# Loads of two, four and two rows per partition in place of four and four, with stores of two rows from the same ring

## The chip, the cores and the metric

One core of one Trainium2 chip runs the kernel. The metric is the device time of one execution in microseconds (us), the median over several runs. All runs in this document are with a granted clock of 1.0. Each kernel was also profiled once. The span in a profile, from the first to the last instruction, is about 1.8 us shorter than the device time. The packet durations below come from this one profiled execution of each kernel.

Terms: HBM is the chip's main memory, SBUF the core's own memory with 128 partitions. A DMA is a transfer between or within them, done by 16 DMA engines. A ring is the queue of transfers that one issuing engine (here SP, or SyncE) fills. A packet is the piece of a transfer that one DMA engine moves at a time, as the trace records it.

## The reference

```python
def reference(x, axis):                      # x: 1024 x 4096, float32; axis = -1
    mean = np.mean(x, axis=axis, keepdims=True)
    return ((x - mean) ** 2).astype(np.float32)
```

The input and the output are 16.78 MB each. Every row of 4096 elements (16 KiB) needs its mean before its first output element can be made.

## The kernel before

The 1024 rows are two tiles of 128 partitions, with four consecutive rows per partition. Both tiles are loaded first, with one DMA each. For each of the four row columns of a tile, VectorE (DVE) makes the negative sum and the negative mean, and ScalarE (ACT) squares x minus the mean in place. After every two rows a store goes out. All loads and stores are issued by SP, so they stand in one ring.

```python
x_t = x.rearrange("(n p q) d -> n p (q d)", p=P, q=Q)       # Q = 4, two tiles
out_t = out.rearrange("(n p q) d -> n p (q d)", p=P, q=Q)
...
for i in range(ntiles):
    x_tile = io.tile([P, Q * D], F32)
    nc.sync.dma_start(out=x_tile, in_=x_t[i])
...
        nc.vector.reduce_sum(out=neg_sum, in_=row, ..., negate=True)
        nc.vector.tensor_scalar_mul(out=neg_mean, in0=neg_sum, scalar1=inv_d)
        nc.scalar.activation(out=row, in_=row, func=Square, bias=neg_mean, scale=1.0)
        if q % H == H - 1:                                   # H = 2
            part = slice((q + 1 - H) * D, (q + 1) * D)
            nc.sync.dma_start(out=out_t[i][:, part], in_=tiles[i][:, part])
```

## Time and profile before

| | before |
|---|---|
| device time, median (lowest to highest) | 83.22 us (83.12 to 83.38, 3 runs; with a fourth run 83.19 us) |
| span | 81.3 us |
| DVE, ACT busy | 35.4 us, 30.7 us |
| DMA queue, share of 16 engines' span | 96.2% |
| first reduction starts | 22.50 us |
| first store issued | 39.46 us |
| loads landed | 22.5 and 41.8 us |

The share of the queue is the row to look at first. The prediction below shows the lines themselves. One more view is needed for what follows: the loads by their tensor. Its last line gives the time from issue to landing, as minimum, median and maximum over the loads. Before:

```profile
L43 SPq DMA_DIRECT2D x_tile<-in_x_dram x2: 382/404/425, 0.7 to 1.2; - x2
DMA to landing us min/median/max: 21.7/31.2/40.6
```

The second load is issued at 1.16 us and lands 40.6 us later, at 41.8 us. In the trace all load packets start before the first store packet does, so this moment is where the loads end and the stores begin.

### The profile page before, as it was taken

The page shows a single profiled execution, that of the slowest core. Times are in us where ns is not written, and L with a number is a line of the kernel's source. Part 1 is how long each engine was busy: PE and PEld are TensorE (multiplying, and loading weights), DVE is VectorE, ACT ScalarE, POOL GpSimd, SP SyncE. Part 2 cuts the span into 40 slices and gives each one's busy share as a digit, 9 for nine tenths or more (in the row PEclk, how much of TensorE's full clock was granted, in tenths as well). Part 3 has the DMA queues.
Part 4 walks back from the last instruction along what each step waited for, and adds up shares of the span by engine and source line. Part 5 has one row for each costly group of instructions (what it writes and reads, how often), then busy time and mean ns, then how long its engine had stood idle before and what let it go on. Part 6 is the DMA issues. An engine that isn't in the chain of part 4 may idle for free.

```text
span 81.3 us, 79 instructions
## 1 busy us (share of the span) xinstructions
DVE 35.4 (44%) x16; ACT 30.7 (38%) x9; POOL 0.2 (0%) x4
## 2 busy tenths in 40 slices
DVE  0000000000099999999749999999920000000000
ACT  0000000000060005969699930979879980000000
POOL 0000000000000000000000000000000000000000
DMA  9399947999965999992997997997998998898990
GB/s 387 129 516 516 516 193 322 516 516 516 516 290 226 516 516 516 516 483 129 419 516 306 467 516 322 451 516 338 435 516 354 419 516 387 387 516 387 403 500 0
DMA packets 864, 33.55 MB, mean 413 GB/s; under 512 B 96, under 2 KB 96, under 8 KB 96
## 3 DMA queue, kind: packets, MB, share of 16 engines
q1 hardware_dynamic: 864, 33.55, 96.2%
HBM read 16.78 MB, written 16.78 MB: 412 GB/s over the span
## 4 chain that ended last, share of the span: by engine, by line
DMA 50%; DVE 22%; ACT 5%; ACTq 4%; SPq 0%; issue 0%
DMA x_tile<-in_x_dram 50%; DVE neg_sum L51 21%; ACT x_tile L55 5%; ACTq L95 4%; SPq L43 0%; DVE neg_mean L54 0%
## 5 line engine op out<-in xcount | busy, mean ns | idle before, releaser
L51 DVE TENSOR_REDUCE neg_sum<-x_tile 128x1 f32<-128x4096 f32 x8 | 35.0, 4413 | 24.1 <-DMA x_tile<-in_x_dram 24.1
L55 ACT ACTIVATE x_tile<-x_tile,neg_mean 128x4096 f32<-128x4096 f32 x8 | 29.4, 3704 | 13.5 <-DVE neg_mean L54 13.5
L55 ACT ACT_TABLE_LOAD x1 | 1.3, 1283 | 22.5 <-DMA x_tile<-in_x_dram 22.5
L54 DVE TENSOR_SCALAR neg_mean<-neg_sum 128x1 f32<-128x1 f32 x8 | 1.1, 148 | 0.0
L81 POOL MEMSET const-bfloat16-1.0<- 128x1 bf16 x1 | 0.1, 101 | 0.0
L81 POOL MEMSET const-uint8-127<- 128x1 uint8 x1 | 0.1, 101 | 0.0
L81 POOL MEMSET const-float32-0.0<- 128x1 f32 x1 | 0.1, 98 | 0.2 <-issue 0.2
L81 POOL MEMSET const-float32-1.0<- 128x1 f32 x1 | 0.1, 98 | 0.0
## 6 DMA issues: line engine op xcount, KB each, us to landing
out_dram<-x_tile SPq DMA_DIRECT2D x4, 4096.0 KB, 12.9
x_tile<-in_x_dram SPq DMA_DIRECT2D x2, 31.2
```

The source lines that it names most:

```text
L51: nc.vector.reduce_sum(out=neg_sum, in_=row, axis=mybir.AxisListType.X, negate=True)
L54: nc.vector.tensor_scalar_mul(out=neg_mean, in0=neg_sum, scalar1=inv_d)
L55: nc.scalar.activation(out=row, in_=row, func=mybir.ActivationFunctionType.Square, bias=neg_mean, scale=1.0,)
L81: nc = _bacc.Bacc("TRN2", target_bir_lowering=False, num_devices=1)
L95: with _tile.TileContext(nc) as tc:
```

## The change

The intent is to let the engines start earlier: with a first load of half the size, DVE has its first two rows in half the time. The rows are laid out anew to make that possible. A partition now owns eight consecutive rows (a pitch of 128 KiB), of which the loads take two, four and two.

```diff
-    Q = 4
-    H = 2
+    R = B // P
+    LOADS = [2, 4, 2]
+    S = 2
...
-    x_t = x.rearrange("(n p q) d -> n p (q d)", p=P, q=Q)
+    x_v = x.rearrange("(p r) d -> p (r d)", p=P)
...
+    for i, n in enumerate(LOADS):
+        x_tile = io.tile([P, n * D], F32, tag=f"x{i}")
+        nc.sync.dma_start(out=x_tile, in_=x_v[:, r0 * D:(r0 + n) * D])
+        rows += [(x_tile, k) for k in range(n)]
+        r0 += n
...
+        if r % S == S - 1:
+            nc.sync.dma_start(
+                out=out_v[:, (r + 1 - S) * D:(r + 1) * D],
+                in_=x_tile[:, (k + 1 - S) * D:(k + 1) * D],
             )
```

(The sum, the mean and the square of each row are as before.)

More of the change, by code (lines that the diff above doesn't have):

```diff
@@ L27 @@
     P = nc.NUM_PARTITIONS
-    Q = 4
-    H = 2
-    assert B % (P * Q) == 0
-    ntiles = B // (P * Q)
+    R = B // P
+    LOADS = [2, 4, 2]
+    S = 2
+    assert B == P * R and sum(LOADS) == R
     inv_d = 1.0 / float(D)
-    x_t = x.rearrange("(n p q) d -> n p (q d)", p=P, q=Q)
-    out_t = out.rearrange("(n p q) d -> n p (q d)", p=P, q=Q)
-    io = ctx.enter_context(tc.tile_pool(name="io", bufs=ntiles))
-    stats = ctx.enter_context(tc.tile_pool(name="stats", bufs=2 * ntiles * Q))
-    tiles = []
@@ L41 @@
-    for i in range(ntiles):
-        x_tile = io.tile([P, Q * D], F32)
-        nc.sync.dma_start(out=x_tile, in_=x_t[i])
-        tiles.append(x_tile)
-    for i in range(ntiles):
-        for q in range(Q):
-            row = tiles[i][:, q * D:(q + 1) * D]
-            neg_sum = stats.tile([P, 1], F32)
-            neg_mean = stats.tile([P, 1], F32)
-            nc.vector.reduce_sum(
-                out=neg_sum, in_=row, axis=mybir.AxisListType.X, negate=True
-            )
-            nc.vector.tensor_scalar_mul(out=neg_mean, in0=neg_sum, scalar1=inv_d)
-            nc.scalar.activation(
-                out=row,
-                in_=row,
-                func=mybir.ActivationFunctionType.Square,
-                bias=neg_mean,
-                scale=1.0,
-            )
-            if q % H == H - 1:
-                part = slice((q + 1 - H) * D, (q + 1) * D)
-                nc.sync.dma_start(out=out_t[i][:, part], in_=tiles[i][:, part])
+    x_v = x.rearrange("(p r) d -> p (r d)", p=P)
@@ new lines @@
+    out_v = out.rearrange("(p r) d -> p (r d)", p=P)
+    io = ctx.enter_context(tc.tile_pool(name="io", bufs=1))
+    stats = ctx.enter_context(tc.tile_pool(name="stats", bufs=2 * R))
+    rows = []
+    r0 = 0
+    for i, n in enumerate(LOADS):
[3 more added lines that the diff above has]
+        r0 += n
+    for r, (x_tile, k) in enumerate(rows):
+        row = x_tile[:, k * D:(k + 1) * D]
+        neg_sum = stats.tile([P, 1], F32)
+        neg_mean = stats.tile([P, 1], F32)
+        nc.vector.reduce_sum(
+            out=neg_sum, in_=row, axis=mybir.AxisListType.X, negate=True
+        )
+        nc.vector.tensor_scalar_mul(out=neg_mean, in0=neg_sum, scalar1=inv_d)
+        nc.scalar.activation(
+            out=row,
+            in_=row,
+            func=mybir.ActivationFunctionType.Square,
+            bias=neg_mean,
+            scale=1.0,
+        )
+        if r % S == S - 1:
+            nc.sync.dma_start(
+                out=out_v[:, (r + 1 - S) * D:(r + 1) * D],
+                in_=x_tile[:, (k + 1 - S) * D:(k + 1) * D],
+            )
```

## The prediction

> **What bounds the kernel now.** I read the page first: the engines' busy time, the DMA row of the 40 slices, and the queue.
>
> ```profile
> span 81.3 us, 79 instructions
> ...
> DVE 35.4 (44%) x16; ACT 30.7 (38%) x9; POOL 0.2 (0%) x4
> ...
> DMA  9399947999965999992997997997998998898990
> ...
> q1 hardware_dynamic: 864, 33.55, 96.2%
> HBM read 16.78 MB, written 16.78 MB: 412 GB/s over the span
> ```
>
> No compute engine is busy for half of the span; the one DMA queue is busy for 96.2% of it. The low digits in the DMA row look like pauses, but a digit counts a large packet in the slice where it was recorded, so neighbouring digits trade with each other. To see whether the pauses are real I cut the span at the moments when the traffic starts, changes from loads to stores and ends, and then the store half into pieces of one store each (window; then its length and the busy time of DVE, ACT and POOL; the last three numbers are the TensorE clock, the DMA share and GB/s):
>
> ```profile
> 1.83:41.50 39.67, 17.71 (x8) 10.09 (x4) 0.00 (x0) 1.00 1.00 430
> 41.50:80.20 38.70, 17.71 (x8) 20.64 (x6) 0.00 (x0) 1.00 0.97 420
> ...
> 41.50:51.20 9.70, 9.37 (x4) 6.45 (x3) 0.00 (x0) 1.00 1.00 432
> 51.20:60.90 9.70, 8.34 (x5) 8.34 (x3) 0.00 (x0) 1.00 1.00 432
> 60.90:70.60 9.70, 0.00 (x0) 5.85 (x2) 0.00 (x0) 1.00 1.00 432
> ```
>
> The pauses are gone: the DMA share is 1.00 from the first byte to 70.6 us, at 430 to 432 GB/s. The packet records of the trace say the same: 256 load packets of 64 KiB (median 2.418 us) and 512 store packets of 32 KiB (median 1.213 us). All their times, summed and divided by 16 engines, are 78.2 us, and the traffic runs from 1.83 to 80.2 us, 78.4 us. The transfers fill the span with next to no hole.
>
> Then I read the chain of waits, which seems to say otherwise:
>
> ```profile
> 1.16 40.64 DMA x_tile<-in_x_dram
> ...
> 41.83 8.75 DVE neg_sum L51 x2
> ...
> 59.45 3.71 ACT x_tile L55
> 63.15 3.60 ACTq L95
> ```
>
> It is a chain through the second load, the four reductions of the second tile and the last squares. But it ends at 66.8 us, 14.5 us before the span does: the landing of the last stores is not in it. The waits of SP's own queue have it: at the end of the kernel SP stands 13.3 us for the stores.
>
> ```profile
> SPq L95 <- DMA out_dram<-x_tile: 13.3, 2, 9.6
> ```
>
> So what matters of the engine chain is one thing only: does each store reach the queue before the queue runs dry? The timeline of SP, taken store by store, gives the issue time and the time to landing:
>
> ```profile
> 39.46 0.35 SPq L64 DMA_DIRECT2D out_dram<-x_tile  x1
> DMA to landing us min/median/max: 12.1/12.1/12.1
> 47.45 0.34 SPq L64 DMA_DIRECT2D out_dram<-x_tile  x1
> DMA to landing us min/median/max: 13.8/13.8/13.8
> 58.79 0.33 SPq L64 DMA_DIRECT2D out_dram<-x_tile  x1
> DMA to landing us min/median/max: 12.1/12.1/12.1
> 66.78 0.33 SPq L64 DMA_DIRECT2D out_dram<-x_tile  x1
> DMA to landing us min/median/max: 13.8/13.8/13.8
> ```
>
> The landings are at 51.6, 61.3, 70.9 and 80.6 us, one every 9.7 us, although the issues are 8.0, 11.3 and 8.0 us apart. A store of 4.19 MB that takes 9.7 us moves at 432 GB/s; the even landings under uneven issues show a queue that always has work. Each store was issued before its predecessor had landed: by 2.4 us (the second load landed at 41.83), 4.1, 2.5 and 4.1 us. **The bound is the bytes in the one ring**, not the engines and not a wait.
>
> **What the Trainium skill says.** "DMA: Bandwidth & Descriptors", section "Where 436 GB/s comes from", puts the ceiling of the 16 engines at 435.2 GB/s; the 432 GB/s of the store windows agree, so there is hardly any rate left to win. The same page, section "Queues, rings and completion order", says that on each DMA engine descriptors are consumed in ring order. The trace agrees: no store packet starts before the loads of its engine are through, though the first store is issued 2.4 us earlier. The same page, section "Latency and other measured facts", gives copies that slow down as the row pitch in HBM goes up in powers of two: 207 GB/s each way at 512 KiB against 214 when full, 164 at 2 MiB. The trace before has a pitch of 64 KiB and shows no loss; the new pitch is 128 KiB, which the page does not list. "Perfetto Trace Analysis", section "DMA Instruction — HWDGE (DVE, Sync)", says that the data movement is outside the profiled window of a DMA instruction. Here a store issue lasts 0.33 us and its data land 12 to 14 us later, which is why the chain of waits stops short.
>
> **The change, part by part.**
>
> 1. **Loads.** The same 16.78 MB, in three instructions instead of two: two rows (32 KiB a partition), four (64 KiB), two. Per DMA engine 16 packets of 64 KiB become 8 of 64 KiB and 16 of 32 KiB. Before: 16 x 2.418 = 38.69 us. After: 8 x 2.418 + 16 x 1.213 = 38.75 us. That is +0.06 us on the path, and one more round of semaphore packets, 9 ns each. One more issue on SP takes 0.4 us (two took 0.86), beside 10 us of queued data: nothing.
>
> 2. **First landing.** Of the first load's 8 packets per engine half the bytes go: 8 x 1.209 = 9.7 us less, so it lands at 22.5 - 9.7 = 12.8 us. The second lands 19.3 us later (41.83 - 22.50 is that step before) at 32.2, the third at 41.9 us. DVE and ACT start 9.7 us sooner.
>
> 3. **Stores.** The same four of 4.19 MB with packets of 32 KiB, from the same ring: 32 x 1.213 = 38.8 us per engine, unchanged. I replayed their issue times with the instruction order of the changed build, which is R0 R1 T0 T1 R2 R3 T2 R4 T3 R5 T4 R6 T5 R7 T6 T7 on DVE (R a reduction, T the small multiply): T5 stands behind R6, so row 5 waits for the third load. The durations are those of before: first R to first square 8.84 us (22.50 to 31.34), a further row every 4.39 us (31.34 to 35.73), a square 3.71 us, two squares back to back 7.31 us.
>  - Store 1: 12.8 + 8.84 + 7.31 = 29.0 us (before 39.46). The loads hold the ring until 41.9, so it waits behind them: 12.9 us ahead.
>  - Store 2: 32.2 + 8.84 + 4.39 + 3.71 = 49.1 us (before 47.45). Needed at about 51.7, when store 1 has landed: 2.6 us ahead.
>  - Store 3: rows 4 and 5 begin at 49.8 and 54.2, as the third load has long landed; 54.2 + 3.7 = 57.9 us (before 58.79). Needed at 61.4: 3.5 us ahead.
>  - Store 4: the last reduction ends at 58.5; 58.6 + 7.3 = 65.9 us (before 66.78). Needed at 71.0: 5.1 us ahead.
>
> The queue never runs dry in this replay. The tightest is store 2; an issue needs about 1.1 us to its first bytes (the first issue is at 0.73 us, the first packet at 1.83), so about 1.5 us stay.
>
> 4. **Layout.** Each partition now owns eight consecutive rows of 16 KiB, a pitch of 128 KiB, and the ring reads pieces of 32 or 64 KiB out of it. Bytes and packet sizes otherwise stay; I put nothing for it in the sum.
>
> **Sum:** 38.75 + 38.8 us of packets against 38.69 + 38.8, hence +0.06 us; start and end as before. 83.22 + 0.06 is **83.3 us**.
>
> **The rivals.**
>
> *The early start is worth its 9.7 us.* This is the evident intent: the idle view shows 22.5 us in which DVE waits for the first load. For it speaks the chain of waits, in which the load is 50% of the span. It would make some 73.5 us. Against it: the same 33.55 MB at 432 GB/s need 77.7 us by themselves, so no start of the engines gets below about 81 us with the 1.8 us before and the rest after the traffic.
>
> *The last store sets the end.* If the end followed the issue of the last store, it would come 0.9 us sooner (65.9 for 66.78): 82.3 us, still within 2%. Against it: that store is issued 4.1 us before its predecessor lands.
>
> *A store comes late.* Only if the reductions or squares ran slower, or the load landed some 1.5 us later than replayed, would the ring be empty before store 2. Every microsecond beyond that would be added: perhaps 84 us. DVE and ACT took the same time per instruction under full traffic in the kernel before (4409 to 4421 ns; 3692 to 3709 ns), which speaks against it.
>
> *The wider pitch slows HBM.* The skill's first listed step, 207 for 214, is 3%; at a quarter of that pitch I expect less. The full 3% on 78 us would be +2.4 us, 85.6 us. Only this rival can reach the slower verdict.
>
> **Range and chances.** The centre is the sum. The runs before span 83.12 to 83.38. Below, the floor of bytes allows a few tenths at most (a shorter start with smaller first packets): 82.8. Above, a late store or a trace of the pitch: 84.0. Faster by over 2% would be under 81.6 us, which the bytes all but exclude: 0.02. Slower by over 2% is over 84.9 us, by the pitch: 0.05. Within 2%: 0.93.
>
> **What would show each step right or wrong.** In the profile after, the queue should have 1008 packets (384 of loads, 512 of stores, 112 of semaphores), 33.55 MB, a share near 96%, and the DMA share should be 1.00 at 430 GB/s in windows from the first packet to the last store. The first reduction should start near 12.8 us; the stores should be issued near 29.0, 49.1, 57.9 and 65.9 and still land near 51.7, 61.4, 71.0 and 80.7 us, with about 22.7 us from issue to landing for the first. DVE's and ACT's waits before the end should be longer in the middle, SP's last wait for the stores some 14 us. I would be wrong if the packets of 32 or 64 KiB took clearly longer than 1.213 and 2.418 us (the pitch), if a hole opened before a store (the replay), or if store packets ran among the loads (the ring order).

## The result, and the profile after

| | before | after |
|---|---|---|
| device time, median (lowest to highest) | 83.19 us (83.12 to 83.38, 4 runs) | 84.41 us (84.27 to 84.47, 4 runs) |
| ratio to before, 95% interval | | 1.0141 (1.0119 to 1.0163) |
| span | 81.3 us | 82.6 us |
| first reduction starts | 22.50 us | 12.80 us |
| stores issued | 39.46, 47.45, 58.79, 66.78 us | 28.97, 49.10, 57.88, 65.86 us |
| stores landed | 51.6, 61.3, 70.9, 80.6 us | 52.8, 62.4, 72.1, 81.8 us |

A ratio is the mean time of one kernel's runs over the mean of the other's runs of the same rounds, so it is not quite the ratio of the medians in the table. The change is 1.2 us slower. By the 2% rule that still counts as the same, but it is far outside the noise, and outside the predicted range (82.8 to 84.0 us).

The page after, the lines that answer to those of before:

```profile
span 82.6 us, 83 instructions
...
DMA  8698990999999099799879998997998999799790
...
q1 hardware_dynamic: 1008, 33.55, 96.1%
HBM read 16.78 MB, written 16.78 MB: 406 GB/s over the span
```

The queue is as busy as before, 96.1% of a longer span. It has the 1008 packets that were predicted, and it moves the same bytes in more time. So either all packets became a little slower, or a few of them much slower. The stores by their tensor, the first and the last of them (issue, then issue to landing):

```profile
28.97 0.35 SPq L64 DMA_DIRECT2D out_dram<-x_tile  x1
DMA to landing us min/median/max: 23.8/23.8/23.8
...
65.86 0.33 SPq L64 DMA_DIRECT2D out_dram<-x_tile  x1
DMA to landing us min/median/max: 15.9/15.9/15.9
```

The issue times are the replayed ones to within 0.1 us. All landings are 1.1 us late against the replay (52.8 for 51.7, 81.8 for 80.7), the first one as much as the last. The time was therefore lost before the first store landed, and never again. The loads by their tensor, after:

```profile
L44 SPq DMA_DIRECT2D x_tile<-in_x_dram x3: 383/424/426, 0.7 to 1.6; - x3
DMA to landing us min/median/max: 12.0/31.0/41.4
```

The first two loads land at 12.7 and 32.1 us, as predicted. The third is issued at 1.6 us and lands 41.4 us later, at 43.0 us and not at 41.9. The loss is in the third load. Windows from the first packet to 38.65 us, from there over the end of the loads to 43 us, and the rest (columns as in the prediction: the last number is GB/s) place it. First before, then after:

```profile
1.75:38.65 36.90, 16.15 (x6) 7.91 (x3) 0.00 (x0) 1.00 1.01 430
38.65:43.00 4.35, 2.73 (x4) 3.67 (x2) 0.00 (x0) 1.00 1.01 437
```

```profile
1.75:38.65 36.90, 15.44 (x6) 8.59 (x3) 0.00 (x0) 1.00 1.00 425
38.65:43.00 4.35, 4.35 (x3) 2.02 (x1) 0.00 (x0) 1.00 1.08 362
```

In the 4.35 us around the end of the loads the rate falls from 437 to 362 GB/s, while the DMA share does not fall (1.01 and 1.08; a window can show more than 1, and the bytes of a packet count in one piece): the engines are "busy" with packets that take longer. The 425 for 430 GB/s in the first window means nothing, since experiment 2, which loses no time, has 425 as well. The packet records show which. Sorted by their start, every 16 successive data packets are taken as one round, one packet on each engine (the records do not name the engine). Rounds are numbered from 0; round 0, in which the traffic starts, is left out:

| round of the kernel after | starts | mean duration |
|---|---|---|
| 1 to 7 (first load, 32 KiB) | 3.6 to 11.2 us | 1.211 to 1.213 us |
| 8 to 15 (second load, 64 KiB) | 12.1 to 29.3 us | 2.418 to 2.424 us |
| 16 to 21 (third load, 32 KiB) | 31.4 to 37.8 us | 1.213 us |
| 22 (third load) | 38.7 to 39.0 us | **1.720 us** |
| 23 (third load) | 40.2 to 40.9 us | **1.760 us** |
| 24 to 55 (all stores, 32 KiB) | 42.0 to 80.2 us | 1.213 us |

Two rounds, the last two of the loads, lose 0.507 + 0.547 = 1.05 us, and in both of them all 16 packets took longer than 1.213 us. With the predicted 0.06 us for the smaller packets that is 1.11 us. The rest of the 1.2 us goes with a wider scatter: the last 16 load packets end within 0.68 us of each other, before within 0.50 us. In the kernel before, the last load round (64 KiB) took 2.429 us, 0.01 more than the others.

Why those two? Nothing else in the timeline begins there. Three things differ between the kernels at that moment: a store has been in the ring since 28.97 us (before: only since 39.46 us, 2.3 us ahead of the loads' landing), the last load packets are of 32 KiB, and the layout is new.

### The profile page after: what moved, and what is told of

The parts are those of the page before. It is cut to its first block, busy times and chain, and to the rows that moved or that the text cites. A ratio compares the mean times of both kernels' runs of the same rounds, so it can differ in the third digit from the quotient of the medians.

```text
span 82.6 us, 83 instructions
## 1 busy us (share of the span) xinstructions
DVE 35.4 (43%) x16; ACT 30.7 (37%) x9; POOL 0.2 (0%) x4
## 2 busy tenths in 40 slices
DMA packets 1008, 33.55 MB, mean 406 GB/s; under 512 B 112, under 2 KB 112, under 8 KB 112
## 3 DMA queue, kind: packets, MB, share of 16 engines
q1 hardware_dynamic: 1008, 33.55, 96.1%
## 4 chain that ended last, share of the span: by engine, by line
DMA 37%; DVE 32%; ACT 4%; ACTq 4%; SPq 0%; issue 0%
DMA x_tile<-in_x_dram 37%; DVE neg_sum L52 32%; ACT x_tile L56 4%; ACTq L98 4%; SPq L44 0%; DVE neg_mean L55 0%
## 5 line engine op out<-in xcount | busy, mean ns | idle before, releaser
L56 ACT ACT_TABLE_LOAD x1 | 1.3, 1283 | 12.8 <-DMA x_tile<-in_x_dram 12.8
```

The lines of the kernel that those rows point to most:

```text
L56: nc.scalar.activation(out=row, in_=row, func=mybir.ActivationFunctionType.Square, bias=neg_mean, scale=1.0,)
```

## The experiments

**The theory:** a store that already stands in the ring slows the last load packets ahead of it. **The rivals:** the wider pitch in HBM, the smaller load packets, or the third load. Four kernels tell these apart; each is the changed kernel with one edit.

### 1. The layout alone

```diff
-    LOADS = [2, 4, 2]
+    LOADS = [4, 4]
```

> The changed kernel with two loads of four rows again, so that only its row layout (eight consecutive rows per partition, 128 KiB pitch) is left of the change. Theory (the last load packets slow down because a store already waits in the ring behind them): the first store is issued near 39.5 us again, the last load packets take about 2.43 us, the time is 83.2 us. Rival layout (the wider pitch slows HBM): about 84.4 us, with slow packets somewhere among the loads.

Measured: 83.19 us against 83.25 for the kernel before, ratio 0.9988 (0.9973 to 1.0003). The first store was issued at 39.52 us, and the last load round took 2.427 us. The layout, with its pitch of 128 KiB, costs nothing.

### 2. The changed kernel with a late first store

```diff
+    HOLD = 3
+    W = D - 256
+    scratch = io.tile([P, W], F32, tag="scratch")
...
+        if r == S - 1:
+            for _ in range(HOLD):
+                nc.scalar.activation(out=scratch, in_=row[:, :W], func=Square,
+                                     bias=neg_mean, scale=1.0)
         nc.scalar.activation(out=row, in_=row, func=Square, ...)
```

> The changed kernel with three idle squares of 3840 columns into a scratch tile ahead of the second row's square, in ScalarE's idle time, so that the first store is issued near 39.8 us, not 28.97; loads, layout, packets and all later stores as in the changed kernel. Theory of the store that waits too early: the last two rounds of load packets take 1.21 us again, not 1.72 and 1.76, and the time falls to about 83.3 us. Rivals (packets of 32 KiB at the end of the loads; three loads in flight; the layout): 84.4 us, unchanged.

Measured: 83.03 us against 83.25, ratio 0.9975 (0.9957 to 0.9993). Below are its first store, then the landing of its loads, then the window over the end of the loads:

```profile
39.52 0.35 SPq L77 DMA_DIRECT2D out_dram<-x_tile  x1
...
DMA to landing us min/median/max: 12.0/30.9/40.2
...
38.65:43.00 4.35, 4.35 (x3) 2.90 (x2) 0.00 (x0) 1.00 1.10 475
```

The third load now lands 40.2 us after its issue instead of 41.4, and the window has 475 GB/s instead of 362. (This number and the 437 of before are not to be compared finely: a window counts a packet's bytes in one piece, and the packets differ in size.) Rounds 22 and 23 took 1.213 us each. Loads, packets, layout and the stores 2 to 4 are those of the changed kernel. **Adding work to the kernel, three idle squares, took the whole 1.2 us away**, because it held the first store back by 10.5 us. The quarter of a per cent by which it is under the kernel before is no gain that I would claim: its profiled span is 81.5 us against 81.3.

### 3. Large last packets, early store

```diff
-    LOADS = [2, 4, 2]
+    LOADS = [2, 2, 4]
```

> The changed kernel with loads of two, two and four rows: the last load packets are 64 KiB again, but the first store is still issued near 29 us and the second near 38.7 us, both well before the loads end. Theory of the early store: the loss stays, about 1.1 us in the last load packets, 84.3 us. Rival (32 KiB packets at the end of the loads are what slows): gone, 83.2 us.

Measured: 84.37 us, ratio 1.013 (1.0115 to 1.0146). The first store was issued at 28.90 us. The last load round, of 64 KiB packets, took 3.572 us instead of 2.418: the loss is 1.15 us in one packet. The three rounds before it were slower by 0.02 to 0.05 us each, which no other run with an early store showed so clearly. Small packets are not the cause; about the last 64 KiB of each engine's loads suffer, in whatever packets they come.

### 4. Small last packets and three loads, late store

```diff
-    LOADS = [2, 4, 2]
+    LOADS = [4, 2, 2]
```

> The changed kernel with loads of four, two and two rows: the last load packets are 32 KiB as in the changed kernel, there are three loads, but the first store is issued near 39.5 us. Theory of the early store: no loss, 83.2 to 83.4 us. Rival (32 KiB packets at the end of the loads, or a third load): 84.4 us.

Measured: 83.31 us, ratio 0.9998 (0.9980 to 1.0016). The first store was issued at 39.63 us, and no load round after the first was slow. Neither the third load nor small packets at the end cost anything. Of the three differences only the early store is left, and experiment 2 shows that taking it away is enough.

### 5 and 6. How early is too early?

The kernel of experiment 2 with less idle work, so that the first store comes a few microseconds earlier:

```diff
# experiment 5
-    HOLD = 3
-    W = D - 256
+    HOLD = 2               # of whole rows, D columns
# experiment 6
-    W = D - 256
+    W = D - 776
```

> As the late-first-store run, but with two idle squares of full width, so that the first store is issued near 36.4 us. Theory of a limited look-ahead (the loss comes about when the store is in the ring before the last 64 KiB of each engine's load, which begin near 38.7 us): the whole loss, 84.4 us, last two load rounds 1.72 and 1.76 us. Rival (the loss grows with the time for which the store waits in the ring): about a quarter of it, 83.5 us.

> As the late-first-store run, but with the idle squares cut to 3320 columns, so that the first store is issued near 38.2 us, some 0.5 us ahead of the last two load rounds; with about 1.1 us from issue to first bytes it becomes visible to the engines near 39.3 us. Theory of a limited look-ahead: a part of the loss, mainly in the last round, 83.5 to 84.2 us. Rival (a matter of waiting time): below a tenth, 83.3 us.

| first store issued | round 22 | round 23 | loss in both | device time | ratio (interval) |
|---|---|---|---|---|---|
| 28.97 us (the change) | 1.720 | 1.760 | 1.05 us | 84.41 us | 1.0141 (1.0119 to 1.0163) |
| 36.51 us (5) | 1.321 | 2.146 | 1.04 us | 84.42 us | 1.0137 (1.0115 to 1.0160) |
| 38.35 us (6) | 1.213 | 1.833 | 0.62 us | 83.92 us | 1.0085 (1.0068 to 1.0101) |
| 39.52 us (2) | 1.213 | 1.213 | none | 83.03 us | 0.9975 (0.9957 to 0.9993) |

The loss does not grow with the time in the ring: 7.5 us more or less of waiting make no difference. What counts is whether the store is there when the engines get to the last two rounds. At 36.51 us the loss is whole, though it does not fall on the two rounds as expected (1.321 and 2.146 us in place of 1.72 and 1.76). At 38.35 us, 0.2 us ahead of round 22 (its packets start from 38.53 us on), that round is untouched and the next one loses 0.62 us. At 39.52 us, nothing is lost. The step lies within 3 us of issue time.

### 7, 9 and 10. How much of a store?

The kernel of experiment 2, with a small first piece of row 0 stored early by a DMA of its own (issued near 25.4 us); the rest of the first store still comes near 39.5 us.

```diff
+        E = 128            # experiment 7: 512 B per partition; 9: E = 512; 10: E = 1024
+        if r == 0:
+            nc.sync.dma_start(out=out_v[:, 0:E], in_=x_tile[:, 0:E])
         if r % S == S - 1:
+            e = E if r == S - 1 else 0
             nc.sync.dma_start(
-                out=out_v[:, (r + 1 - S) * D:(r + 1) * D],
+                out=out_v[:, (r + 1 - S) * D + e:(r + 1) * D],
                 ...                      # and the same in in_
```

> As the late-first-store run (rest of the first store near 39.5 us), but the first 128 columns of row 0 (512 B per partition, 4 KiB per engine) are stored by a DMA of their own, issued near 25.3 us and waiting in the ring. Theory that the loss is work done ahead in proportion to the store's bytes: nearly nothing, 83.1 to 83.3 us (8 more packets of 512 B per engine and one semaphore round included). Rival (any store behind the loads costs the turn): the whole loss, 84.3 us or more, with the last two load rounds near 1.7 us.

> As the tiny-early-store run, with 512 columns (2 KiB per partition, 16 KiB per engine) in the early store. Theory of data taken ahead (the engine fetches store data early while loads are still to be written, up to about 30 KB per engine, which is the lost 1.1 us at 27 GB/s, and the write side never gets that time back): about half of the loss, 0.6 us, 83.7 us. Rival (the loss needs large store packets, or comes from the store that is issued near 39.5 us alone): 83.1 to 83.2 us as with 512 B.

> The same with 1024 columns (4 KiB per partition, 32 KiB per engine) in the early store. Theory of data taken ahead: the whole loss or nearly, 1.0 to 1.2 us, 84.1 to 84.3 us, with the last two load rounds slow. Rival: 83.1 to 83.3 us.

| early store, per engine | loss in rounds 22 and 23 | its bytes at 32 KiB per 1.213 us | device time | ratio (interval) |
|---|---|---|---|---|
| 4 KiB (7) | under 0.01 us | 0.15 us | 83.12 us | 0.9982 (0.9966 to 0.9999) |
| 16 KiB (9) | 0.62 us | 0.61 us | 83.99 us | 1.0098 (1.0067 to 1.0128) |
| 32 KiB (10) | 1.09 us | 1.21 us | 84.42 us | 1.0137 (1.0119 to 1.0155) |
| 256 KiB (the change) | 1.05 us | 9.7 us | 84.41 us | 1.0141 (1.0119 to 1.0163) |

So it is not the mere presence of a store in the ring: one of 4 KiB per engine is free. The loss grows with the bytes of the early store, at 16 KiB by just the time which an engine takes to move them, and it stops growing somewhere between 16 and 32 KiB per engine (a loss of 1.05 to 1.09 us, at 32 KiB per 1.213 us, would be 28 to 29 KiB: an estimate). The early store has 8 packets per engine in all three, so it is not their number that counts. Against experiment 7 the device time of experiments 9 and 10 rises by some 0.2 to 0.3 us more than the rounds lose, so that both lie above what was expected (83.99 for 83.7 us, 84.42 for 84.1 to 84.3 us). The packet records of both have about 0.3 us more of pauses than those of experiment 7, around the short packets of the early store.

### 8. The first store in another ring

```diff
-            nc.sync.dma_start(
+            ring = nc.scalar if r == S - 1 else nc.sync
+            ring.dma_start(
```

> The changed kernel with the first store alone in ScalarE's ring, so that from about 30 us it runs among the loads instead of behind them; the third load then lands near 51 us and the stores 3 and 4 are issued near 59.6 and 67.6 us, still ahead of need. Theory that an engine loses whenever it handles store data beside load data: the loss is multiplied by the packets mixed, several us, 86 us or more. Rival (the loss belongs to a turn in one ring alone): 83.3 us.

Both theories missed here. Measured: 84.26 us, ratio 1.0127 (1.0107 to 1.0147). Below are the queues of its page, then the landing of its loads:

```profile
q1 hardware_dynamic: 864, 29.36, 84.5%
q10 hardware_dynamic: 144, 4.19, 11.8%
...
DMA to landing us min/median/max: 12.0/31.6/50.8
```

The store ran among the loads: the third load landed at 52.4 us, the store (issued at 28.88 us, landed 23.7 us later) at 52.6. The load round under way when the store arrived took 2.963 us instead of 2.418, the next round (still of loads alone) 1.610 and the first mixed one 1.230 instead of 1.213. That is 0.96 us, nearly all of it ahead of the first store packet, which starts at 33.5 us. After that, the other 13 rounds in which loads and store are mixed took 1.213 us each. Mixing is not what costs. The loss is paid **once, just before the first store packets start among the loads**, at about the same size as in one ring.

### 11 and 12. Is it the write to HBM?

The kernel of experiment 2 with a copy of one row per partition within SBUF, in the ring early (11) or just ahead of the first store (12).

```diff
+    copy = io.tile([P, D], F32, tag="copy")
...
+        if r == 0:                                                 # 12: r == 1
+            nc.sync.dma_start(out=copy, in_=rows[0][0][:, 0:D])    # 12: D:2 * D
```

> As the late-first-store run, with a copy of row 0 from SBUF to a spare SBUF tile (16 KiB per partition, 2.1 MB in all) issued near 25.3 us, so that it waits in the ring behind the loads; the first store is issued near 39.6 us behind it. The copy itself adds about 4.9 us to both this and the next run. If the loss comes from reading SBUF ahead of the loads' end: the last two load rounds are slow and this run is about 1.1 us slower than the next. If it takes a write to HBM: load rounds of 1.21 us and the same time as the next.

> The same copy (of row 1) issued near 39.5 us, just ahead of the first store: the control. Load rounds of 1.21 us in every theory; about 88 us.

The landing of the loads, for experiment 11 and then 12:

```profile
DMA to landing us min/median/max: 12.1/31.0/41.5
```

```profile
DMA to landing us min/median/max: 12.0/30.9/40.2
```

With the early copy the third load lands 1.3 us later than with the late one. Its last two rounds took 1.921 and 1.745 us; with the late copy they took 1.21 us. So the loss needs no write to HBM: a queued transfer that reads SBUF is enough. The comparison of the total times did not come out as expected: 89.29 us (11) against 90.26 us (12, expected 88), the early copy being faster. The late copy's own packets of 16 KiB took 0.833 us (median) against 0.611 us in the early one, 8 x 0.22 = 1.8 us over all, more than the loads lost. I did not find out why. It may have to do with the same fetching ahead, or with the row copied. The control is therefore no control for the total time, only for the load rounds.

## Why the prediction was wrong

**The steps that held.** The bound was named rightly: the bytes in the DMA engines, not the engine chain. The start of the first reduction (12.8 us), the four issues (29.0, 49.1, 57.9 and 65.9 us), the packet count and the packet sizes came out to within 0.1 us or exactly. The queue never ran dry: the packets still fill all but 0.4 us of the traffic (79.3 of 79.7 us). One reading was slightly off without effect: the first packet before starts at 1.75 and not at 1.83 us, so an issue needs about 1.0 us to its first bytes. The 0.06 us for smaller packets is in the records (1.213 us for 32 KiB against half of 2.418). The rival of the early start, 9.7 us of gain, got nothing, as argued; the rival of the late store did not occur. The rival of the pitch, the only one that I gave a chance to slow the kernel by over 2%, was false: experiment 1 has the pitch and no loss.

**The step that failed** is the one on the first store in part 3: "The loads hold the ring until 41.9, so it waits behind them: 12.9 us ahead." The sum counted this wait as free, and the early issue only as margin. In fact a store which waits behind the loads is not idle. It lengthened the last two load rounds by 1.05 us, and everything behind them moved by as much. The sum lacked this term; the others were right. That the time still lies within 2%, to which I gave 0.93, is luck as far as the mechanism goes: nothing in the sum bounded this loss. I had even listed slower packets as a sign that I was wrong, but tied it to the pitch alone.

**What the runs showed in its place.** Shown: the cause is that the store is in the ring well before the loads land (at 41.8 us without a loss): 2.3 us ahead cost nothing, 3.4 us a part and 5.3 us the whole (experiments 2, 6 and 5, with the layout and the packet sizes cleared by 1, 3 and 4). The loss grows with the bytes of the early transfer up to about 30 KiB per engine (7, 9, 10). It is paid once (8, and the store rounds of 1.213 us after). A queued transfer that reads SBUF is enough, without a write to HBM (11). Not every queued transfer does it: loads queued behind loads, which read HBM, cost nothing where one load follows another (rounds 7 and 15 of the changed kernel, 1.213 and 2.424 us).

Argued, not shown: the engine fetches the data of the queued store while its last loads are still to be written. The Trainium skill, "DMA: Bandwidth & Descriptors", section "Two DMAs through the same engine are not ordered", says that descriptors of one queue start in order but are pipelined, and that the read and the write side of an engine are separate queues. That allows it, and it was open to me when I took ring order to mean that the store does nothing until its turn. If the read side gives its time to the store for some 30 KiB, the write side gets its loads that much later. At 27 GB/s per engine (32 KiB in 1.213 us), 30 KiB are 1.1 us, which is the loss. The write side was already at its full pace, so it can't catch up; in the trace the store packets indeed keep their 1.213 us and the 1.1 us stay lost. The records have one more sign of a change of state. In every run with the loss in one ring (the change, 3, 5, 6, 9, 10 and 11) all 32 KiB packets that start after 43 us take exactly 1.213 us. In every run without it some take longer: 5.2% before, 6.0, 6.0, 22.9, 40.6 and 81.8% in experiments 1, 2, 4, 7 and 12, up to 1.262 us. In experiment 8 they are even until the packets of store 2 end, at 61.3 to 61.9 us, and uneven from store 3 on, which was issued only at 60.70 us. A read side that has got ahead once, and loses its lead when the queue runs short, would do that; no run shows the lead itself. The idea fits the dose of experiments 9 and 10, but not quite that of 7, where 4 KiB should have cost 0.15 us and cost nothing. Why a load's reads should wait for those of a store behind it, why the fetched data do not shorten the first store, and why the late copy of experiment 12 was slow stay open too.

**And the intent of the change?** The 9.7 us by which the engines start earlier had no worth, since the ring was full before and after. Their one effect on the time was to bring a store into the ring 10.5 us earlier, and that was the harm. No version here beats the kernel before by more than a quarter of a per cent: it moves 33.55 MB at 430 GB/s, with the traffic filling all but 3 us of the span.

## What to carry to other kernels

When one DMA ring is busy from end to end, earlier compute buys nothing; check first that the traffic has a hole to fill. A transfer that waits in a queue is not free of effect: here a store of 16 KiB or more per engine, queued behind loads some 3 us or more before they ended, cost 0.6 to 1.1 us once, and issuing it 2.3 us before the end cost nothing. When all the landings shift by the same amount, look for the first packets that took longer, not at the end of the chain.

## What the Trainium skill lacked or had wrong

- "DMA: Bandwidth & Descriptors", section "Queues, rings and completion order": it tells of the ring order and that later writes may overtake, but not that a store waiting in the ring slows the loads ahead of it. Here it did by 1.05 us, over the last two rounds of load packets (1.720 and 1.760 us instead of 1.213), with the whole loss for an early store of 32 KiB per engine and 0.62 us for one of 16 KiB.
- The same page, section "Issuing engines are not separate DMA queues", says that transfers of several issuing engines interleave, which experiment 8 agrees with (13 mixed rounds at 1.213 us). It doesn't have the one-time loss of 0.96 us just before the store's first packets.
- The same page, section "Latency and other measured facts", begins its list of row pitches, taken with copies between HBM tensors, at 512 KiB. A pitch of 128 KiB cost nothing here (83.19 us against 83.25).
- No page says that the pace of a copy within SBUF can depend on when it is queued: 16 KiB packets took 0.611 us when the copy was queued early and 0.833 us (median) when queued late, unexplained.
